# A hybrid decoder step on one core: weights loaded one unit earlier, and margins for steps in the planner of the side chains

## The chip, the cores and the metric

One core of a Trainium2 chip runs the whole program. The metric is the device time of one execution in microseconds, the median of several runs. The engines are TensorE (PE, with its weight loads shown apart as PEld), VectorE (DVE), ScalarE (ACT), GpSimd (POOL) and SyncE (SP), which issues all DMAs of this kernel in one queue.

## The reference

One step of a one-layer recurrent decoder is computed for 2048 prompt tokens and for 8 samples of 4 tokens, with 1024 channels, all in float32:

```
u   = LN(x) @ w_in                       # columns for four head groups
A: gated DeltaNet   (conv, delta rule, a triangular solve in each chunk)
B: Mamba-2 SSD      (conv, scalar decay)
C: HGRN2            (a decay per channel)
D: mLSTM            (running-max stabiliser)
h   = LN(alpha * x + concat(A, B, C, D) @ w_out)
out = LN(alpha * h + relu(h @ w_up)^2 @ w_down)
```

The recurrences A to D carry a state along the tokens and give it out at the end. All of it is exactly causal.

## The kernel before, in words

**The main line of work.** The prompt is cut into 4 blocks of 512 tokens; the 32 sample tokens ride along with block 0 in the input projection and with block 2 in the rest. `do_P` multiplies by w_in, block after block; `do_W` by w_out; `do_F` by w_up and w_down. Float32 accuracy comes from a split: weights and activations are each a high and a low half (fp32r), and three products are summed, high x high, low x high, high x low. A *unit* is 512 x 128 weights, 256 KB; there are 832 units. `w_get` issues the load of a unit into one of four `wraw` buffers, `w_split` makes its halves `whi` (mostly on ACT) and `wlo` (on POOL or DVE) in four buffers each, and `gemm` runs 4 x 3 matmuls with them (twice as many with sample tokens). `w_pump`, called before each unit, keeps loads and splits ahead: loads up to unit `cur + 4`, splits up to `cur + 2`.

**The side chains.** Beside the main line run generators, and each `yield` in them ends a step. `mix_stream("a")` runs `gen_A` for chunk after chunk of 128 tokens, `mix_stream("b")` runs `gen_B`, `gen_C`, `gen_D` in turn; `ln` streams make the layer norms and load the mixed results (`y_pre`); and each finished projection has an evacuating generator (`u_conv`, `u_gate` and others). A job of a mix stream begins in `begin`, with the loads of its inputs (`laA`, `laC`, `kzA`, `kzD`); the next job can begin at the mark `"pre"` of the one before it.

In `gen_A`, the inverse of 32 x 32 diagonal blocks is made by 31 steps on POOL (`a`, then `x32`), each with a row of the block that is broadcast to all partitions. The rows go to DRAM (`ud32d`) and come back in eight loads of four rows each into two `nb` buffers (`fetch`). After them, a product with the mask `bd32` on DVE puts the result into `X`, and PE transposes `X`. In `gen_C`, `level` runs for seven sizes in a staggered way: differences of the log decays on DVE, an exponential on ACT, products `qz` (in `kzD`) and `e_` on DVE, and a matmul of the two on PE.

**What sets the order.** The program is written out in one order by a planner, and each engine runs its queue in that order. The planner is the class `_Sim`: it holds a clock for each engine, estimates the time of each instruction when it is written, and knows when each tile is ready by this estimate; `move` does the same for a DMA, with one issue after another and a time to land. `gemm` calls `R.tick()` after every third matmul (or pair). `tick` lets a generator make its next step if its `ready` time is not later than PE's clock plus a slack (both slacks are negative, -0.25 and -0.3). `ready` is the latest estimated end of what the generator's last step wrote; `R.hold(us)` puts it later. Streams make no step while DVE's or ACT's clock is more than `BACK` (2.0) us ahead of PE's. `R.until` lets the chains go on without the main line, where the main line needs their result.

`tvp(n, late)` chooses POOL for an operation if POOL's estimated end is before the later of DVE's estimated end and PE's clock plus `late`; `cpv` chooses between ACT and DVE in the same way. In `w_split` they are called with `LATE_W` and `LATE_W - 1.0`, where `LATE_W` is 5.0.

The lines that record an instruction are one helper's (L341), so the profile's groups tell instructions apart by their tiles; DMAs have L470.

Of the kernel before, what the change touches and what calls it, by code (L numbers as in the profile page):

```python
# [39 lines left out]
EARLY_W = 3  # L40
SLACK = -0.25
SLACK_E = -0.3
BACK = 2.0
LATE_W = 5.0
LATE_U = 3.0
LN1_PACE = 0.1
W0_AT = 29
# [202 lines left out]
class _Run:  # L250
# [56 lines left out]
    def tick(self, fast=False):  # L307
        self.moved = False

        def ok(g, slack):  # L310
            return fast or g.ready <= self.clock["pe"] + slack
        live, self.evac = self.evac, []
        keep = [g for g in live if not ok(g, SLACK_E) or self._adv(g)]
        self.evac = keep + self.evac
        for q in self.streams.values():
            c = self.clock
            if not fast and max(c["dve"], c["act"]) > c["pe"] + BACK:
                break
# [36 lines left out]
def _ap(x):  # L355
    return x[:] if callable(x.ap) else x
# [85 lines left out]
def kernel(ctx: ExitStack, tc: tile.TileContext, t):  # L442
    nc = tc.nc
    R = _Run()
# [21 lines left out]
    mult, add, sub = ALU.mult, ALU.add, ALU.subtract  # L466
    vmax, vmin = ALU.max, ALU.min

    def dma(out, in_):
        nc.sync.dma_start(out=out, in_=in_)  # L470
        R.op("dma", R.sim.move(_ap(out), _ap(in_)))

    def A(out, in_, func, scale=1.0, bias=0.0):
        S.activation(out=out, in_=in_, func=func, scale=scale, bias=bias)
# [10 lines left out]
    def tt(out, a, b, op, eng=None):  # L485
        (eng or V).tensor_tensor(out=out, in0=a, in1=b, op=op)
# [27 lines left out]
    def bc1(ap, n):  # L514
        a = ap.unsqueeze(1)
        return a.to_broadcast([ap.shape[0], n] + list(ap.shape[1:]))
# [102 lines left out]
    units = []  # L619
    wst = {"nload": 0, "nsplit": 0, "cur": 0, "turn": 0}  # L620
    raws, his = {}, {}

    def w_get(i):
        w = sb4.tile([128, 4, 128], F32, tag="wraw", name="wraw")
        dma(w, units[i])
        raws[i] = w

    def w_pump():
        cur = wst["cur"]
        while wst["nload"] < min(cur + 5, len(units)):  # L630
            i = wst["nload"]
            w_get(i)
            wst["nload"] += 1
            if wst["nsplit"] < min(cur + 3, wst["nload"]):
                w_split()
        while wst["nsplit"] < min(cur + 3, len(units)):
            w_split()

    def w_split():
        i = wst["nsplit"]  # L640
        w = raws.pop(i)
        hi = sb4.tile([128, 4, 128], F32R, tag="whi", name="whi")
        lo = sb4.tile([128, 4, 128], F32R, tag="wlo", name="wlo")
        cpv(hi, w, 512, LATE_W - 1.0)
        tt(lo, w, hi.bitcast(F32), sub, tvp(512, LATE_W))
        his[i] = (hi, lo)
        wst["nsplit"] += 1
# [657 lines left out]
    def pa():  # L1305
        return psa.tile([128, 512], F32, tag="a", name="pa_")
# [16 lines left out]
    def gen_A(m):  # L1323
# [22 lines left out]
        p = pa()  # L1346
# [28 lines left out]
        if not dec:  # L1375
            ud = ta1(4, 32)
            V.tensor_reduce(out=ud, in_=X.rearrange("p h (b r) -> p h r b", r=32), axis=AX.X, op=add)
            V.tensor_copy(x32, bc1(C("id32", 32), 4))
            yield
            dma(ud32d, ud.rearrange("p h r -> p (h r)"))  # L1380
            yield
            rows = ud32d.rearrange("(b k) c -> b k c", k=32)
            nb = {}

            def fetch(q):
                if q < 8:
                    nb[q] = nbp.tile([128, 4, 4, 32], F32, tag="nb", name="nb")
                    dma(nb[q].rearrange("p k h r -> p (k h r)"), rows[:, 4 * q:4 * q + 4].rearrange("b k c -> b (k c)").unsqueeze(1).to_broadcast([4, 32, 512]))

            for q in range(NBUF):  # L1390
                fetch(q)
            yield
            tf = ta1(4, 31)
            for k in range(31):
                w_ = 31 - k
                tt(tf[:, :, 0:w_], nb[k // 4][:, k % 4, :, k + 1:], x32[:, :, k:k + 1].to_broadcast([128, 4, w_]), mult, G)
                tt(x32[:, :, k + 1:], x32[:, :, k + 1:], tf[:, :, 0:w_], sub, G)
                if k % 4 == 3:
                    yield
                if k % 4 == 3:  # L1400
                    fetch(k // 4 + NBUF)
            xb = x32.unsqueeze(2).to_broadcast([128, 4, 4, 32])
            tt(X.rearrange("p h (b r) -> p h b r", r=32), xb, bc1(C("bd32", 128).rearrange("p (b r) -> p b r", r=32), 4), mult, tvp(512))
            yield
# [194 lines left out]
    def gen_C(m):  # L1599
# [14 lines left out]
        p = pb()  # L1614
# [19 lines left out]
        def level(li, s):  # L1634
            e_ = tb1(2, 128)
            for i in range(2):
                evi = e_[:, i, 0:n].rearrange("p (b e s) -> p b e s", e=2, s=s)
                gvi = la[:, 2 + i, 0:n].rearrange("p (b e s) -> p b e s", e=2, s=s)
                gm = gvi[:, :, 0, s - 1]
                tt(evi[:, :, 0, :], bcf(gm, s), gvi[:, :, 0, :], sub, tvp(64))  # L1640
                tt(evi[:, :, 1, :], gvi[:, :, 1, :], bcf(gm, s), sub, tvp(64))
            yield
            ex(e_[:, :, 0:n], e_[:, :, 0:n])
            yield
            qz = kzD[:, :, 64 * (li % 2):64 * (li % 2) + 64].rearrange("p (i h) r -> p i h r", i=2)
            qv = la[:, 0:2, 0:n].rearrange("p i (b e s) -> p i b e s", e=2, s=s)
            ev = e_[:, :, 0:n].rearrange("p i (b e s) -> p i b e s", e=2, s=s)
            for h in range(2):
                sl = slice(64 * h, 64 * h + 64)
                tt(qz[sl, :, h, 0:nh].rearrange("p i (b s) -> p i b s", s=s), qv[sl, :, :, 1, :], ev[sl, :, :, 1, :], mult)  # L1650
            tt(e_[:, :, 0:n], k_, e_[:, :, 0:n], mult)
            yield
            pl = pb()
            for i in range(2):
                if n == 128:
                    mm(pl[:, i * 128:i * 128 + 128], e_[:, i, :], qz[:, i])
                else:
                    for h in range(2):
                        mm(pl[:n, (2 * i + h) * nh:(2 * i + h) * nh + nh], e_[:, i, 0:n], qz[:, i, h, 0:nh])
            yield  # L1660
            pv = pl[:n, 0:4 * nh].rearrange("p (h b s) -> p h b s", h=4, s=s)
            av = at[:n, :, 0:n].rearrange("p h (b e s) -> p h b e s", e=2, s=s)[:, :, :, 1, :]
            if s == 64:
                V.tensor_copy(av[0:64], pv[0:64])
            else:
                mk = bc1(C("lmc", nh, 64 * li, n).bitcast(U32), 4).rearrange("p h (b s) -> p h b s", s=s)
                V.copy_predicated(out=av, mask=mk, data=pv)
# [129 lines left out]

    def mix_stream(which):
        fns = (gen_A,) if which == "a" else (gen_B, gen_C, gen_D)
        jobs = []  # L1800
        for b in range(NB):
            for c, dec in [(c, False) for c in range(CPB)] + ([(0, True)] if b == DECB else []):
                for f in fns:
                    mark = None
                    if f is fns[-1]:
                        if dec:
                            mark = ("x", which)
                        elif c == CPB - 1:
                            mark = (b, which)
                    jobs.append((b, c, dec, f, mark))  # L1810

        def begin(i):
            b, c, dec, f, mark = jobs[i]
            m = chunk(b, c, dec)

            def store(k, y):
                def go(ready):
                    R.cur.ready = ready
                    R.hold(1.0)
                    yield  # L1820
                    dma(m.yT[:, k:k + 2, :], y[:, :, 0:m.n])
                    if mark:
                        done["mix"].add(mark)
                R.start(go(R.cur.ready))

            m.store = store
            g = _Task(f(m))
            g.ready = R.cur.ready
            R._adv(g)
            return g  # L1830

        def fed(i):
            g = {gen_A: "A", gen_B: "B", gen_C: "C", gen_D: "D"}[jobs[i][3]]
            return left[jobs[i][0]][""] == left[jobs[i][0]][g] == 0

        nxt = None
        for i in range(len(jobs)):
            g = nxt
            nxt = None
            if g is None:  # L1840
                while not fed(i):
                    yield
                g = begin(i)
            R.cur.ready = max(R.cur.ready, g.ready)
            yield
            for mark in g.gen:
                if mark == "pre" and i + 1 < len(jobs) and fed(i + 1):
                    nxt = begin(i + 1)
                yield
        if which == "a":  # L1850
            dma(t["pa_ssm"], SA)
        else:
            dma(t["pb_ssm"], SB)
            dma(t["pc_ssm"], SC)
            dma(t["pd_mem"], SD)
# [418 lines left out]
```

## Time and profile before

| | |
|---|---|
| median of 3 runs | 3063.7 us (3060.96 to 3063.87) |
| profiled execution | 3063.81 us |
| its span, first to last instruction | 3061.9 us |
| mean granted TensorE clock | 0.983 |
| busy: PE, PEld | 2889.6 us, 2480.4 us |
| busy: DVE, POOL, ACT | 2141.5 us, 1621.9 us, 1260.7 us |
| instructions: PE, DVE, ACT, POOL | 16668, 4038, 2685, 1993 |
| DMA | 407.12 MB, mean 133 GB/s |
| splits: wlo on POOL, on DVE; whi on ACT, on DVE | 769, 63; 829, 3 |

A busy PE counts the modelled end of each matmul, so it is not PE at its peak. Idle time is the gap before an instruction, put down to what released it; only PE's idle time is certain to be part of the time. The input projection of block 3 ends near 1000 us with the first output projection; the side chains run from about 150 to 2290 us; after that PE has the main line alone but for layer norms.

### The profile page before, as it was taken

Reading aid. Unit: us, or ns where it says so; the run is one execution under the profiler, and the core shown is the slowest. Engines: PE = TensorE matmul, PEld = TensorE weight load, DVE = VectorE, ACT = ScalarE, POOL = GpSimd, SP = SyncE. Lnnn points to the kernel's source line nnn. Section 1 sums busy time; section 2 is a strip of 40 time slices with the busy share of each in tenths; the row PEclk is TensorE's granted clock in tenths of the full one; section 3 lists DMA queues with packets and bytes.
Section 4 is the critical chain, followed back from the end, with each engine's and each line's share of the span. In section 5 each row is a group of like instructions: output and inputs, shape, how many; then the busy total and the mean of one; then the engine's idle time right before and its main releaser. Section 6 shows DMA issues by size and latency. Waiting matters only on the chain.

```text
span 3061.9 us, 48064 instructions
## 1 busy us (share of the span) xinstructions
PE 2889.6 (94%) x16668; PEld 2480.4 (81%) x16668; DVE 2141.5 (70%) x4038; ACT 1260.7 (41%) x2685; POOL 1621.9 (53%) x1993
## 2 busy tenths in 40 slices
PE   7889898999999999999999999999999999999997
PEld 7788677777777787877777778878899999878886
DVE  8677796978897687877778766767684354474445
ACT  4654565574564433333335222333542222432222
POOL 4554756585685464466443654453344444444545
PEclk9899999999999999999999999999999999999999
DMA  5775446456557444345443444444333343333333
GB/s 166 127 172 153 141 147 205 138 157 185 157 144 214 130 134 138 118 135 155 134 145 89 144 127 129 135 141 137 112 109 94 86 119 86 111 112 97 100 93 104
DMA packets 361264, 407.12 MB, mean 133 GB/s; under 512 B 65468, under 2 KB 207804, under 8 KB 361020
## 3 DMA queue, kind: packets, MB, share of 16 engines
q1 hardware_dynamic: 361020, 404.04, 46.3%
q8 instruction: 132, 2.16, 0.3%
q14 instruction: 112, 0.92, 0.1%
HBM read 340.20 MB, written 63.72 MB: 132 GB/s over the span
## 4 chain that ended last, share of the span: by engine, by line
PE 48%; DVE 20%; POOL 11%; DMA 11%; issue 6%; ACT 4%; SPq 1%; POOLq 0%; DVEq 0%; ACTq 0%
PE pd L341 40%; DVE g L341 10%; DMA nb<-ud32d 5%; POOL wlo L341 4%; DVE b L341 4%; POOL a L341 3%; POOL x L341 3%; DVE a L341 2%; ACT g L341 2%; DMA wraw<-in_w_in_u_dram 2%; DVE kzD L341 2%; SPq L470 1%; DMA wraw<-in_w_up_u_dram 1%; DMA prx<-in_a_conv_in_dram 1%; POOL g L341 1%
## 5 line engine op out<-in xcount | busy, mean ns | idle before, releaser
L341 PE MATMUL pd<-g,whi 128*128 128x512 f32 (+2 forms) x8112 | 2243.7, 361 | 21.2 <-ACT g L341 11.3
L341 POOL TENSOR_TENSOR wlo<-wraw,whi 128x512 fp32r<-128x512 f32 x769 | 1066.0, 1394 | 1236.7 <-ACT whi L341 1139.3
L341 PEld LDWEIGHTS pd<-g,whi 128*128 128x128 f32 x8112 | 1395.3, 190 | 223.5 <-ACT g L341 12.4
L341 PE MATMUL pd<-g,wlo 128*128 128x512 f32 (+2 forms) x4056 | 1310.5, 354 | 18.7 <-POOL wlo L341 18.0
L341 PEld LDWEIGHTS pd<-g,wlo 128*128 128x128 f32 x4056 | 723.3, 191 | 114.7 <-POOL wlo L341 27.0
L341 ACT ACTIVATE whi<-wraw 128x512 fp32r<-128x512 f32 x829 | 509.4, 626 | 551.0 <-PE pd L341 249.7
L341 DVE TENSOR_TENSOR g<-g 128x512 fp32r<-128x512 f32 (+5 forms) x371 | 368.7, 997 | 199.0 <-ACT g L341 190.1
L341 ACT ACTIVATE g<-pd 128x512 f32<-128x512 f32 (+1 forms) x342 | 174.1, 527 | 495.9 <-PE pd L341 494.2
L341 DVE TENSOR_TENSOR g<-g,pd 128x512 f32<-128x512 f32 (+2 forms) x288 | 159.5, 570 | 221.7 <-PE pd L341 221.0
L341 POOL TENSOR_TENSOR a<-nb,x 128x124 f32<-128x124 f32 (+30 forms) x496 | 201.7, 407 | 97.9 <-DMA nb<-ud32d 68.8
L341 ACT ACTIVATE g<-g 128x512 f32<-128x512 f32 (+5 forms) x343 | 210.0, 633 | 67.6 <-DVE g L341 60.0
L341 POOL TENSOR_TENSOR x<-x,a 128x124 f32<-128x124 f32 (+30 forms) x496 | 197.2, 398 | 38.9
L341 DVE CAST g<-g 128x512 fp32r<-128x512 f32 (+1 forms) x169 | 173.2, 1025 | 7.8 <-ACT g L341 3.0
L341 ACT ACTIVATE b<-b 128x256 f32<-128x256 f32 (+3 forms) x201 | 81.3, 405 | 166.9 <-DVE b L341 166.2
L341 DVE TENSOR_TENSOR b<-laC 128x64 f32<-128x64 f32 (+2 forms) x471 | 117.4, 307 | 9.6 <-DMA laC<-UC 9.6
L341 DVE SCALAR_TENSOR_TENSOR g<-g 128x512 f32<-128x512 f32 (+3 forms) x124 | 111.5, 905 | 17.7 <-ACT g L341 15.4
L341 DVE SCALAR_TENSOR_TENSOR g<-g,par 128x512 f32<-128x512 f32 (+1 forms) x128 | 117.5, 934 | 1.2 <-ACT g L341 1.1
L341 DVE TENSOR_TENSOR kzD<-laC,b 64x128 f32<-64x128 f32 (+1 forms) x228 | 108.4, 475 | 2.0 <-ACT b L341 0.3
L341 DVE BATCH_NORM_STATS2 bst<-g 128x6 f32<-128x512 f32 (+1 forms) x98 | 65.7, 683 | 44.4 <-ACT g L341 40.9
L341 DVE TENSOR_SCALAR g<-g 128x512 int32<-128x512 int32 (+7 forms) x137 | 72.9, 550 | 32.9 <-ACT g L341 32.1
L341 POOL TENSOR_TENSOR g<-g 128x512 f32<-128x512 f32 (+3 forms) x47 | 70.2, 1497 | 43.7 <-ACT g L341 38.9
L341 DVE TENSOR_TENSOR wlo<-wraw,whi 128x512 fp32r<-128x512 f32 x63 | 52.1, 828 | 53.4 <-ACT whi L341 53.1
(2536 smaller groups left out, 2738.0 us busy)
## 6 DMA issues: line engine op xcount, KB each, us to landing
wraw<-in_w_dn_u_dram SPq DMA_DIRECT2D x264, 256.0 KB
wraw<-in_w_up_u_dram SPq DMA_DIRECT2D x256, 256.0 KB
wraw<-in_w_in_u_dram SPq DMA_DIRECT2D x248, 256.0 KB
nb<-ud32d SPq DMA_DIRECT2D x128, 256.0 KB
wraw<-in_w_out_u_dram SPq DMA_DIRECT2D x64, 256.0 KB
UC<-g SPq DMA_DIRECT2D x40, 256.0 KB
g<-in_x_prompt_dram SPq DMA_DIRECT2D x32, 256.0 KB
hTd<-g SPq DMA_DIRECT2D x32, 256.0 KB
```

What stands on the lines that cost most here:

```text
L341: r = f(*a, **k)
L470: nc.sync.dma_start(out=out, in_=in_)
```

## The change

Six places change, and none of them adds or removes arithmetic.

- `w_pump` loads up to unit `cur + 5` instead of `cur + 4`. The `wraw` buffers stay four.
- `LATE_W` goes from 5.0 to 3.0, so a weight's halves go to DVE where POOL's (ACT's) estimated end is more than 3.0 (2.0) us behind PE's clock, and later than DVE's.
- `dma` can add time to the landing estimate; `fetch` uses it with 3.2 us for the `nb` rows.
- After the 31 steps of `gen_A` stands `R.hold(SWEPT)`, 2.0 us, and one more `yield`, before the product that needs the result.
- In `level` of `gen_C`, `R.hold(BUSY)`, 0.7 us, stands before the step with the matmul.
- In `begin`, the job's `ready` is put 1.5 us (`LOADED`) later after its loads are issued.

```
+LOADED = 1.5
+SWEPT = 2.0
+BUSY = 0.7
-LATE_W = 5.0
+LATE_W = 3.0
...
-    def dma(out, in_):
+    def dma(out, in_, extra=0.0):
         nc.sync.dma_start(out=out, in_=in_)
-        R.op("dma", R.sim.move(_ap(out), _ap(in_)))
+        R.op("dma", R.sim.move(_ap(out), _ap(in_), extra))
...
-        while wst["nload"] < min(cur + 5, len(units)):
+        while wst["nload"] < min(cur + 6, len(units)):
...
-                    dma(nb[q]..., rows[...]...to_broadcast([4, 32, 512]))
+                    dma(nb[q]..., rows[...]...to_broadcast([4, 32, 512]), 3.2)
...
                 if k % 4 == 3:
                     fetch(k // 4 + NBUF)
+            R.hold(SWEPT)
+            yield
             xb = x32.unsqueeze(2).to_broadcast([128, 4, 4, 32])
...
             tt(e_[:, :, 0:n], k_, e_[:, :, 0:n], mult)
+            R.hold(BUSY)
             yield
             pl = pb()
...
             g = _Task(f(m))
             g.ready = R.cur.ready
             R._adv(g)
+            g.ready += LOADED
             return g
```

More of the change, by code (lines that the diff above doesn't have):

```diff
@@ L1387, in fetch @@
                     nb[q] = nbp.tile([128, 4, 4, 32], F32, tag="nb", name="nb")
-                    dma(nb[q].rearrange("p k h r -> p (k h r)"), rows[:, 4 * q:4 * q + 4].rearrange("b k c -> b (k c)").unsqueeze(1).to_broadcast([4, 32, 512]))
+                    dma(nb[q].rearrange("p k h r -> p (k h r)"), rows[:, 4 * q:4 * q + 4].rearrange("b k c -> b (k c)").unsqueeze(1).to_broadcast([4, 32, 512]), 3.2)
             for q in range(NBUF):
```

## The prediction

> **What bounds the kernel now.** I read the page's busy shares first, then a table of busy time by stage, then who waited for whom, engine by engine.
>
> ```profile
> 250.00:950.00 700.00, 653.12 (x3312) 533.57 (x3312) 582.41 (x1109) 406.59 (x847) 447.79 (x578) 0.98 0.55 158
> 950.00:1600.00 650.00, 617.07 (x3302) 508.25 (x3302) 486.62 (x1009) 243.57 (x567) 338.33 (x526) 0.99 0.49 143
> 1600.00:2285.00 685.00, 658.28 (x3895) 555.42 (x3895) 501.58 (x1094) 255.09 (x572) 322.52 (x430) 0.99 0.42 123
> 2285.00:2650.00 365.00, 365.00 (x2748) 356.80 (x2747) 167.12 (x215) 92.35 (x181) 175.35 (x128) 1.00 0.36 105
> ```
>
> Each row is a stretch of the span, with its length, the busy time of PE, PEld, DVE, ACT and POOL in that order, then the granted clock. PE is the bound. After 2285 us, when the side chains are through, it is never idle (365.0 of 365.0). While they run it loses 47, 33 and 27 us in the three stretches. Everything that the change touches lies in those stretches, so its whole scope is PE's waits there and the clock that the waits cost. PE has no slack anywhere: a wait taken off PE comes off the span, one added goes on.
>
> The waits show which steps were put into the engines' queues too early.
>
> ```profile
> PEld pd L341 <- POOL wlo L341: 27.0, 23, 3.3
> POOL a L341 <- DMA nb<-ud32d: 68.8, 28, 6.7
> DVE a L341 <- POOL x L341: 51.5, 15, 8.0
> ACT whi L341 <- DMA wraw<-in_w_up_u_dram: 78.1, 29, 9.2
> ACT whi L341 <- DMA wraw<-in_w_in_u_dram: 69.8, 29, 6.5
> ACT whi L341 <- DMA wraw<-in_w_dn_u_dram: 66.1, 24, 6.8
> ACT whi L341 <- DMA wraw<-in_w_out_u_dram: 24.8, 10, 5.3
> SPq L470 <- POOL wlo L341: 938.9, 414, 9.8
> ```
>
> Each row gives total us, times, longest. POOL stands 68.8 us before a recursion step because the broadcast rows (nb) have not landed; the low weight halves (wlo) that are queued behind it come late, and PE's weight loads wait 27.0 us for them. DVE stands 51.5 us at the product that follows the recursion. ACT stands 238.8 us in 92 waits (the four wraw rows) for weights still on their way. The order of time shows one such case from end to end:
>
> ```profile
> 1401.25 0.40 POOL L341 TENSOR_TENSOR a<-nb,x 128x124 f32<-128x124 f32 x1 [6.72 <-DMA nb<-ud32d]
> ...
> 1404.97 1.26 POOL L341 TENSOR_TENSOR wlo<-wraw,whi 128x512 fp32r<-128x512 f32 x1
> ...
> 1406.28 0.29 PEld L341 LDWEIGHTS pd<-g,wlo 128*128 128x128 f32 x1 [3.32 <-POOL wlo L341]
> ...
> 1406.90 0.63 ACT L341 ACTIVATE whi<-wraw 128x512 fp32r<-128x512 f32 x1 [8.66 <-DMA wraw<-in_w_up_u_dram]
> ```
>
> POOL waits 6.72 us for nb, runs the segment, does wlo only at 1404.97, and PE loses 3.32 us. ACT waits 8.66 us for a weight at the same time.
>
> **The change, part by part.** No arithmetic is added or removed; the order of instructions in the queues changes. All sums are against the profiled execution: 3063.8 us, of which 3061.9 are span; the median of the runs is 3063.7, so no correction is needed.
>
> *Margin of 3.2 us for nb, 2.0 us and one more step after the recursion, and splits moved from POOL to DVE two us sooner.* These three aim at PE's wait for wlo, 27.0 us, and at the transposes after the recursion. With the nb margin the planner puts each segment into POOL's queue up to 3.2 us later; 68.8 us in 28 waits are 2.5 us each, so little should be left, and the wlo behind it come earlier. The transposes' share, and that of the late loads below, is in these rows:
>
> ```profile
> PE pa__22049 L341 <- DVE a L341: 2.8, 1, 2.8
> PE pa__8981 L341 <- DVE a L341: 2.0, 1, 2.0
> PE pa__20962 L341 <- DVE a L341: 1.6, 1, 1.6
> PE pa__10472 L341 <- DVE a L341: 1.1, 1, 1.1
> PE pb__13377 L341 <- DMA laC<-UC: 3.1, 1, 3.1
> PE pb__2960 L341 <- DMA laC<-UC: 2.9, 1, 2.9
> PE pb__12345 L341 <- DMA laC<-UC: 1.3, 1, 1.3
> ```
>
> The first four add up to 7.5 us. Bounds for wlo: nothing gained (0) to all 27.0; I take two thirds, 18, since a margin of 3.2 covers the mean of those waits but not the longest, 6.7. For the transposes 0 to 7.5; I take 6, since the margin of 2.0 alone covers three of the four waits. The cost: each recursion gets later in its chain. That chain hides it (below).
>
> *LOADED, 1.5 us at a job's start.* The last three rows are PE's waits for laC, 7.3 us; a margin of 1.5 takes 1.5 + 1.5 + 1.3 = 4. Bounds 0 and 7.3.
>
> *BUSY, 0.7 us before the level products of gen_C.*
>
> ```profile
> L341 DVE TENSOR_TENSOR kzD<-laC,b x228: 216/290/1429, 251.3 to 2240.1; 64x128 f32<-64x128 f32 x112, 64x32 f32<-64x32 f32 x2
> ...
> its engine sat idle before it (us, times) until:
>   DVE b L341: 31.5, 33
> ...
> PE pb__17982 L341 <- DVE b L341: 2.9, 1, 2.9
> ```
>
> The answer for kzD counts the weight load and the matmul of one product separately, so PE's share of 31.5 us is about half, 16 us in some 17 waits, mean 0.95. A later issue by 0.7 takes at most 17 x 0.7 = 12; I take 10 (bounds 0 and 16).
>
> *The clock after these waits.*
>
> ```profile
> 2041.00:2044.00 3.00, 0.63 (x3) 0.19 (x1) 1.39 (x1) 1.63 (x3) 2.61 (x8) 1.00 0.13 48
> 2044.00:2050.80 6.80, 6.41 (x23) 5.79 (x24) 3.80 (x7) 1.39 (x3) 3.13 (x2) 0.52 0.45 114
> 1350.00:1358.00 8.00, 6.12 (x38) 4.84 (x37) 7.86 (x20) 1.90 (x4) 2.54 (x2) 1.00 0.15 52
> 1358.00:1361.00 3.00, 3.00 (x11) 2.55 (x10) 1.76 (x5) 0.00 (x0) 0.00 (x0) 0.52 0.00 0
> 1644.60:1651.40 6.80, 6.80 (x23) 5.39 (x22) 6.61 (x18) 3.79 (x7) 2.01 (x2) 0.52 0.05 20
> ```
>
> The wait of 2.8 us at 2041 is followed by 6.8 us at a clock of 0.52; so are the waits within 1350 to 1358, all for kzD (3.0 us), and the 2.9 us of pb__17982 before 1644.6 (6.8 us). Half of these 16.6 us, 8, is lost to the clock; with two thirds of the waits gone, 6 come back. Bounds 0 and 8. The Trainium skill, "TensorE: Matmul & The Clock Gate", section "What's actually happening", has the array return to half rate only after about 3.4 us of idle window. By that rule waits this short cost no clock, and the sum below would be 6 us smaller in its gain; the trace disagrees, since between 1350 and 1358 PE was busy 6.12 of 8 us and the clock halved all the same.
>
> *Weights one unit further ahead.* There are four wraw buffers, so the load can't start before the low half four units back is done; what changes is its place in SP's queue, ahead of the other transfers of one unit. It helps where such a transfer held it up, as in ACT's 8.66 us above. Directly PE pays little for it; I take 3 us, bounds 0 and 10 (the price of the other small waits here), as ACT's evacuations come sooner. The price: the transfers of that unit (stores, loads of the chains, nb) now stand behind a load that waits for a later wlo. SP's 938.9 us behind wlo should rise to well over 1500. Bounds 0 and 10; I take 3.
>
> *Splits on DVE.*
>
> ```profile
> L341 POOL TENSOR_TENSOR wlo<-wraw,whi x769: 1255/1297/2282, 15.2 to 3042.2; 128x512 fp32r<-128x512 f32 x193
> L341 DVE TENSOR_TENSOR wlo<-wraw,whi x63: 673/746/1816, 17.5 to 2006.2; 128x512 fp32r<-128x512 f32 x63
> DVE wlo L341 <- ACT whi L341: 53.1, 29, 7.0
> 250.00:950.00 700.00, 290.48 (x752) 141.77 (x752) 19.25 (x24) 230.26 (x158) 0.98 0.55 158
> L341 POOL TENSOR_TENSOR a<-nb,x x496: 207/342/1978, 190.7 to 2042.1; 128x124 f32<-128x124 f32 x6, 128x112 f32<-128x112 f32 x6, 128x100 f32<-128x100 f32 x6, 128x88 f32<-128x88 f32 x6
> ```
>
> I expect 63 to become 120 to 200, at 0.75 us of DVE instead of 1.30 us of POOL. Queued behind it on DVE are PSUM evacuations, and PE waits for those; I take 4 us (bounds: -3, as POOL gets freer, and 50, the rival below). The Trainium skill, "SBUF — State Buffer", section "SBUF: two separate sides", says that a GpSimd operation and a VectorE operation with two SBUF inputs lock each other out for the whole instruction. By that rule a split on DVE frees POOL of only 1.30 - 0.75 = 0.55 us and the term of 18 would be nearer 12, the gain 6 smaller; a maximum of 1978 ns against a median of 342 for the recursion's products agrees with such blocking.
>
> *What hides the longer chains.* The margins lengthen the chains, in the second by up to 7 levels x 0.7 us for 12 jobs = 59 us plus part of 39 x 1.5 = 58 by the sample group.
>
> ```profile
> L470 SPq DMA_DIRECT2D yTx<-b x3: 376/377/378, 1777.5 to 1914.4; - x3
> L470 SPq DMA_DIRECT2D g<-yTx x8: 320/430/528, 1980.8 to 1999.8; - x8
> L470 SPq DMA_DIRECT2D wraw<-in_w_out_u_dram x2: 328/374/419, 2108.6 to 2110.0; - x2
> ```
>
> Its last store is at 1914.4; the projection that needs it starts at 2108.6, and loading it took 20 us. About 170 us of lateness are covered; the chains' end at 2285 has a longer cover still, the PE-only stretch. So I cost it at 0; without cover, each us late would be a us of idle PE.
>
> **Sum.** Gains 18 + 6 + 4 + 10 + 6 + 3 = 47. Costs 3 + 4, and 12 (a quarter of the gain) for waits that come next: where one late input is mended, the next (ACT's evacuation of g) is the one that PE meets, = 19. Net 28: 3063.8 - 28 = 3036 us.
>
> **Rivals.**
> *The gain is larger.* Longer chains thin out DVE in 250 to 950, where it is busy 582 of 700 us; 47 us of PE idle there fall as a whole, not only where a margin is. With half of the 107 us of idle in the three stretches gone plus the clock's 8, 61 us: 3003. For it: DVE's share; against: nothing shortens any operation.
> *The waits only move.* All queues are in order, and each shifted step meets other work. Then some 45 of the 47 come back as new waits: 3062, within 3057 to 3069. For it: most PE waits are single events under 3 us, at many places.
> *DVE becomes the bound: slower.* In 250 to 950 it has 700 - 582.4 = 117.6 us free. A moved split takes 0.83 us plus, by the row, 53.1 / 63 = 0.84 of waiting for its high half: 1.67. From 117.6 / 1.67 = 70 moved there (of 158) it decides. With 100 moved, 167 - 118 = 49 us are added against the 28: 3063.8 + 21 = 3085. Against: the planner moves a split only when its own DVE clock is the earlier one.
> *Chains too late for the third block: slower.* Over 170 us of delay needed, I count at most 117; at 200 us PE would idle 30 us, against the 28: 3066.
>
> **Chances.** Forecast 0.56, larger gain 0.11, waits only move 0.16, DVE bound 0.13, chains late 0.04. A measurement can tell about 0.2%, 6 us, from no change. Faster takes the first two and 0.07 of the third: 0.74; same 0.08; slower 0.18. The likeliest case by itself spans 3015 to 3052; the range of 3000 to 3070 leaves out the far part of the larger gain and most of the DVE case, together about 2 in 10.
>
> **What would show it.** Right: POOL's wait for nb from 68.8 to under 20, DVE's for POOL x from 51.5 to under 20, PEld for wlo from 27.0 to under 12, the kzD row from 31.5 to under 18, ACT for wraw from 238.8 to under 170, DVE splits above 120, SP behind wlo above 1500, the last yTx store between 1950 and 2050. PE busy falls little, its idle time falls. Wrong: DVE above 620 us in 250 to 950, PE waits for DVE g or ACT g in place of wlo, or PE idle before the projection near 2100.

## The result, and the profile after

The changed kernel takes 3031.0 us (median of 4 runs, 3030.7 to 3038.8), the kernel before 3063.6: the ratio is 0.9901, with a 95% interval of 0.9887 to 0.9915. Forecast were 3036 us and 3000 to 3070. The sum came out; several of its terms did not.

The busy shares of the page, and the stretches of the span as they were shown before (length; busy PE, PEld, DVE, ACT, POOL; granted clock):

```profile
PE 2873.8 (95%) x16668; PEld 2472.5 (82%) x16668; DVE 2167.6 (72%) x4104; ACT 1249.1 (41%) x2658; POOL 1592.5 (53%) x1958
...
250.00:950.00 700.00, 664.59 (x3406) 545.54 (x3405) 601.94 (x1151) 411.01 (x863) 430.95 (x547) 0.99 0.58 166
950.00:1600.00 650.00, 619.15 (x3312) 513.48 (x3311) 499.46 (x1076) 249.88 (x573) 332.72 (x546) 0.98 0.48 139
1600.00:2285.00 685.00, 664.19 (x4068) 565.34 (x4067) 511.81 (x1055) 243.55 (x543) 335.15 (x434) 1.00 0.44 127
```

The profiled execution spans 3028.4 us after 3061.9, so 33.5 less. PE's idle time went from 3061.9 - 2889.6 = 172.3 to 3028.4 - 2873.8 = 154.6, so 17.7 of the 33.5 is idle time; the other 15.8 us is time in which PE counted as busy, though it ran the same 16668 matmuls. The granted clock accounts for at most about 7 us of that (0.017 x 3062 = 52 us were lost to it before, 0.015 x 3028 = 45 after); the rest was not traced. Between 250 and 950 us, PE is idle for 35 us in place of 47.

The waits, in the order of the rows shown before; the first two rows are PE's own waits for wlo, before and after:

```profile
PE pd L341 <- POOL wlo L341: 18.0, 16, 2.9
PE pd L344 <- POOL wlo L344: 3.7, 4, 1.4
PEld pd L344 <- POOL wlo L344: 6.1, 7, 1.8
PEld pd L344 <- DVE wlo L344: 3.2, 3, 1.9
POOL a L344 <- DMA nb<-ud32d: 71.9, 39, 5.0
DVE a L344 <- POOL x L344: 2.6, 3, 1.6
ACT whi L344 <- DMA wraw<-in_w_up_u_dram: 23.5, 11, 4.6
ACT whi L344 <- DMA wraw<-in_w_in_u_dram: 21.1, 8, 6.4
ACT whi L344 <- DMA wraw<-in_w_out_u_dram: 4.1, 1, 4.1
SPq L473 <- POOL wlo L344: 1226.3, 484, 8.4
```

PE's weight loads wait 6.1 us for wlo from POOL, not 27.0, and PE itself 3.7 us, not 18.0. ACT's waits for weights on their way fell from 238.8 us to 48.7 in these rows (51.0 with w_dn). DVE's stand before the product after the recursion, 51.5 us, is gone; the planner now gives 4 of the 16 products to POOL. POOL's wait for nb, which the nb margin was to remove, is as long as before, 71.9 us against 68.8. And SP stands behind wlo for 1226 us in place of 939, as the deeper loads have it, though not for the "well over 1500" that was forecast.

### The profile page after: what moved, and what is told of

It reads as the page before. It is cut to its first block, busy times and chain, and to the rows that moved or that the text cites. A ratio compares the mean times of both kernels' runs of the same rounds, so it can differ in the third digit from the quotient of the medians.

```text
span 3028.4 us, 48058 instructions
## 1 busy us (share of the span) xinstructions
PE 2873.8 (95%) x16668; PEld 2472.5 (82%) x16668; DVE 2167.6 (72%) x4104; ACT 1249.1 (41%) x2658; POOL 1592.5 (53%) x1958
## 5 line engine op out<-in xcount | busy, mean ns | idle before, releaser
L344 POOL TENSOR_TENSOR wlo<-wraw,whi 128x512 fp32r<-128x512 f32 x710 | 992.7, 1405 | 1218.5 <-ACT whi L344 1089.9
L344 PEld LDWEIGHTS pd<-g,whi 128*128 128x128 f32 x8048 | 1380.6, 189 | 206.6 <-DVE g L344 9.1
L344 ACT ACTIVATE whi<-wraw 128x512 fp32r<-128x512 f32 x813 | 498.8, 626 | 363.0 <-PE pd L344 257.4
L344 DVE TENSOR_TENSOR g<-g 128x512 fp32r<-128x512 f32 (+5 forms) x364 | 357.2, 985 | 177.0 <-ACT g L344 163.5
L344 POOL TENSOR_TENSOR a<-nb,x 128x124 f32<-128x124 f32 (+30 forms) x496 | 199.0, 401 | 101.6 <-DMA nb<-ud32d 71.9
L344 POOL TENSOR_TENSOR x<-x,a 128x124 f32<-128x124 f32 (+30 forms) x496 | 208.2, 420 | 38.9
L344 DVE CAST g<-g 128x512 fp32r<-128x512 f32 (+1 forms) x178 | 187.0, 1051 | 10.2 <-POOL g L344 3.2
L344 DVE TENSOR_TENSOR wlo<-wraw,whi 128x512 fp32r<-128x512 f32 x122 | 95.9, 787 | 55.9 <-ACT whi L344 55.4
L344 DVE SCALAR_TENSOR_TENSOR g<-g 128x512 f32<-128x512 f32 (+3 forms) x124 | 99.5, 805 | 18.9 <-ACT g L344 18.5
```

The source lines that it names most:

```text
L344: r = f(*a, **k)
```

## The experiments

The kernel before was run beside every one; the ratios are to it, and the times are medians. The last four columns are totals of waits in the profile, in us: DVE for POOL's recursion result (x), POOL for nb, ACT for wraw, PEld for wlo from POOL.

| kernel | us | ratio, 95% interval | DVE: x | POOL: nb | ACT: wraw | PEld: wlo |
|---|---|---|---|---|---|---|
| before | 3061.5 to 3064.3 | 1 | 51.5 | 68.8 | 238.8 | 27.0 |
| before, slack -0.27 | 3095.8 | 1.0114 (1.0096 to 1.0132) | 65.5 | 98.0 | 238.2 | 37.1 |
| + load depth | 3096.6 | 1.0104 (1.0085 to 1.0124) | 73.1 | 88.9 | 77.6 | 38.4 |
| + LATE_W | 3132.0 | 1.0218 (1.0192 to 1.0243) | 74.3 | 101.2 | 226.9 | 18.9 |
| + LOADED, BUSY | 3086.9 | 1.0075 (1.0053 to 1.0098) | 50.2 | 48.9 | 244.4 | 23.8 |
| + recursion margins | 3046.0 | 0.9937 (0.9918 to 0.9955) | 0.4 | 13.2 | 149.8 | 17.2 |
| the same, slack -0.27 | 3032.6 | 0.9902 (0.9884 to 0.9919) | 0.4 | 18.8 | 155.3 | 17.7 |
| changed | 3031.0 | 0.9901 (0.9887 to 0.9915) | 2.6 | 71.9 | 51.0 | 6.1 |
| changed, slack -0.27 | 3024.7 | 0.9881 (0.9863 to 0.9898) | 2.5 | 50.8 | 41.7 | 4.1 |
| - load depth | 3037.8 | 0.9921 (0.9905 to 0.9936) | 4.8 | 34.5 | 165.0 | 10.7 |
| - recursion margins | 3130.0 | 1.0229 (1.0209 to 1.0249) | 86.4 | 152.5 | 69.6 | 23.1 |
| - SWEPT alone | 3032.2 | 0.9897 (0.9882 to 0.9913) | 27.0 | 53.8 | 44.2 | 8.2 |
| - nb margin alone | 3055.9 | 0.9971 (0.9956 to 0.9987) | 9.7 | 127.2 | 93.8 | 18.5 |
| changed, nb margin 4.8 | 3003.7 | 0.9805 (0.9788 to 0.9821) | 2.8 | 45.9 | 69.6 | 6.1 |

DVE can wait only for the products that the planner leaves on it: all 16 in the kernels without the hold and in the last one, 7 to 13 in the others.

### One part at a time, on the kernel before

**Load depth alone.**

```diff
-        while wst["nload"] < min(cur + 5, len(units)):
+        while wst["nload"] < min(cur + 6, len(units)):
```

> The kernel before with one edit: loads five units ahead of the running one in place of four. Theory A (most of the 32 us comes through the weights: ACT's waits for wraw fell from 238.8 us to under 60, PE's for wlo from 27.0 to 6.1): 3044 us, between 3036 and 3052; ACT's waits for wraw under 100 us, PEld's for wlo under 15, and the second chain ends before 2284. Theory B, the prediction's split of the gain (3 of 47 us for this part): 3061 to 3066, and SP's longer waits behind wlo show no gain. Theory C (any new order of the same work moves the time by several us either way): no tie between ACT's waits for wraw and the time.

Measured: 3096.6 us, 32 slower. ACT's waits for wraw fell as theory A said, to 77.6 us, and the time rose all the same; the waits of PEld for wlo rose:

```profile
PEld pd L341 <- POOL wlo L341: 38.4, 34, 3.2
POOL a L341 <- DMA nb<-ud32d: 88.9, 42, 5.9
DVE a L341 <- POOL x L341: 73.1, 16, 8.7
```

So ACT's waits for weights do not set the time by themselves, and theory A falls; theory C's "no tie" holds. Theory B's near zero did not come either, but 32 us is no more than an edit that means nothing costs this kernel (below), so they can't be put down to the loads. The second chain ended later, not sooner.

**LATE_W alone.**

```diff
-LATE_W = 5.0
+LATE_W = 3.0
```

> The kernel before with LATE_W 3.0 in place of 5.0 alone. Theory A: 3050 to 3058, wlo on DVE above 100 and PEld's waits for wlo under 18 us. Theory B: a third of the 18 us, 3056 to 3060, less the 4 us for DVE. Theory C: anything from 3054 to 3072.

Measured: 3132.0 us, 68 slower, outside what all three theories gave. The splits moved as expected, 118 wlo on DVE, and PEld's waits for wlo fell to 18.9, just above theory A's 18; but POOL stood 101.2 us for nb and DVE 74.3 us for x, and PE's own waits for DVE's tiles (a, b, g) rose from 59.8 to 119.1 us.

**The recursion's margins alone.**

```diff
-                    dma(nb[q]..., ...to_broadcast([4, 32, 512]))
+                    dma(nb[q]..., ...to_broadcast([4, 32, 512]), 3.2)
...
                     fetch(k // 4 + NBUF)
+            R.hold(2.0)
+            yield
```

> The kernel before with the nb margin of 3.2 and the hold with the extra step after the recursion, alone. Theory B: 3045 to 3052, POOL's waits for nb from 68.8 us to under 20, PEld's for wlo under 15. Theory A: 3058 to 3066; POOL's waits for nb stay near 70 us as they did with the whole change, DVE's waits for POOL x go from 51.5 us to under 10, without a gain on PE.

Measured: 3046.0 us, 18 faster: the one part that gains by itself, in theory B's range.

```profile
PEld pd L341 <- POOL wlo L341: 17.2, 18, 2.1
POOL a L341 <- DMA nb<-ud32d: 13.2, 14, 2.7
...
L341 DVE TENSOR_TENSOR a<-x,con x12: 673/682/1741, 256.0 to 2042.5; 128x512 f32<-128x512 f32 x12
```

POOL's waits for nb fell to 13.2 us as the prediction had it; PEld's for wlo, 17.2, stayed above theory B's 15. The third row is the product after the recursion (min/median/max ns); four of the 16 went to POOL.

**LOADED and BUSY alone.**

```diff
             tt(e_[:, :, 0:n], k_, e_[:, :, 0:n], mult)
+            R.hold(0.7)
...
             R._adv(g)
+            g.ready += 1.5
```

> The kernel before with LOADED 1.5 and BUSY 0.7 alone. Theory B: 14 us for the two plus their clock, 3047 to 3053, the waits of the kzD answer from 31.5 us to under 18. Theory A: 3056 to 3064; the kzD waits fall by half, and others rise.

Measured: 3086.9 us, 23 slower, outside both. The kzD answer has 36.8 us of waits for DVE b, more than the 31.5 of before.

### Is it only the order that was drawn?

The four groups of edits give +32, +68, -18 and +23, a sum of +105, and together -32. So either the parts need each other, or each order is a draw. To tell these apart, an edit that means nothing was run on both kernels.

**The streams' slack, on the kernel before.**

```diff
-SLACK = -0.25
+SLACK = -0.27
```

> The kernel before with the streams' slack at -0.27 in place of -0.25: no margin that means anything, but about 60% of the listed PE rows change place. Theory C: 10 us or more away from 3064, either way. Theory D and the prediction's: within 6 us of 3064, since no step's margin is changed by more than 0.02 us.

Measured: 3095.8 us, 34 slower. An edit of 0.02 us in the planner's arithmetic costs as much as the whole change gained. That is theory C for the kernel before. Its 3064 us look like a favourable order: the five other kernels without the recursion's margins take 3087 to 3132.

**The same edit on the changed kernel.**

> The changed kernel with the streams' slack at -0.27 in place of -0.25. Theory C: 10 us or more away from 3031, and rather slower, if the changed kernel's order is a lucky draw. Theory D: within 6 us of 3031.

Measured: 3024.7 us, 6 faster. This other order cost the changed kernel nothing; neither theory C's "rather slower" nor its 10 us hold.

**The changed kernel without the deeper loads.**

```diff
-        while wst["nload"] < min(cur + 6, len(units)):
+        while wst["nload"] < min(cur + 5, len(units)):
```

> The changed kernel with the load depth put back (four units ahead), all else as changed. The single edits gave +32 us (load depth), +68 (LATE_W), -18 (recursion), +23 (begin and level margins), a sum of +105 where the whole gave -32, so the parts are not additive. Theory D (the parts need each other: the deeper loads take ACT's waits for wraw from 238.8 us to about 80 whatever else is changed, and this pays once the recursion's margins keep POOL free): without the loads 3060 or more, ACT's waits for wraw above 180 us. Theory C (each new order draws a time from a spread of some 20 us, whatever the edit): anything between 3025 and 3090, with no tie to ACT's waits.

Measured: 3037.8 us, ACT's waits for wraw back at 165.0. Theory D's 3060 fails, and so does its 180: some 7 us hang on the load depth here, about what the slack alone moved.

**The changed kernel without the recursion's margins.**

```diff
-                    dma(nb[q]..., ...to_broadcast([4, 32, 512]), 3.2)
+                    dma(nb[q]..., ...to_broadcast([4, 32, 512]))
...
-            R.hold(SWEPT)
-            yield
```

> The changed kernel without the nb margin and without the hold and step after the recursion. Theory D: 3075 or more, DVE's waits for POOL x back above 40 us, POOL's for nb above 85, PEld's for wlo above 20. Prediction's split: 24 us of the gain lost plus clock, 3055 to 3062. Theory C: anything between 3025 and 3090.

Measured: 3130.0 us, 99 slower than with them.

```profile
PEld pd L341 <- POOL wlo L341: 23.1, 16, 3.7
POOL a L341 <- DMA nb<-ud32d: 152.5, 72, 6.5
DVE a L341 <- POOL x L341: 86.4, 16, 10.3
```

All of theory D's signs for this run came, and the time lies outside theory C's spread and the prediction's split. The nb and x rows are back, larger than before; PEld's for wlo, 23.1, stays a little under its 27.0. DVE's mean wait at the product is 86.4 / 16 = 5.4 us, and everything behind it on DVE waits along. PE is idle for 60.6 us more than in the changed kernel. Some 28 us of that are its waits for the transposes right behind the product (31.9 against 3.4), 13 its waits for wlo, and 20 its waits for DVE's b, the tiles of the second chain.

### Which of the two margins

**Without the hold and step after the recursion.**

```diff
-            R.hold(SWEPT)
-            yield
```

> The changed kernel without the hold and step after the recursion; the nb margin stays. Theory E (the price is paid by DVE standing at the product until POOL has ended the recursion, 51 to 86 us in every kernel without the two margins and under 5 in every one with them, and the nb margin does most of it, since it adds up over eight loads): 3028 to 3050, DVE's waits for POOL x under 25 us. Theory G (the step after the recursion does it): 3070 to 3110, DVE's waits for POOL x above 40. Theory C (a drawn order): no tie to DVE's waits for POOL x.

Measured: 3032.2 us, the same as with it; DVE's waits for x are 27.0 us, just above theory E's 25. This speaks against theory E's mechanism: all 16 products are on DVE here, with a median of 1724 ns, DVE stands 24 us more than in the changed kernel, and the time is the same.

**Without the nb margin.**

```diff
-                    dma(nb[q]..., ...to_broadcast([4, 32, 512]), 3.2)
+                    dma(nb[q]..., ...to_broadcast([4, 32, 512]))
```

> The changed kernel without the nb margin; the hold and step after the recursion stay. Theory E: 3075 to 3125, DVE's waits for POOL x above 35 us and POOL's for nb above 100. Theory G: 3028 to 3050, DVE's waits for POOL x under 20. Theory C: as before, no tie.

Measured: 3055.9 us, 25 slower than the changed kernel; between theory G's 3028 to 3050 and theory E's 3075 to 3125, which asked for DVE waits above 35 where there were 9.7 (nine of the 16 products went to POOL). So each of the two alone takes most of the 99 us (98 and 74). The nb margin takes both waits down (nb from 152.5 to 53.8, x from 86.4 to 27.0); the hold takes down DVE's (to 9.7) and little of POOL's (to 127.2). The faster of the two is the one in which DVE stands longer, so the time does not follow DVE's standing by itself. Theory E had the nb margin's place right and its exclusive share wrong.

**The recursion's margins alone, with the other slack.** The edit of the third run above, and `SLACK = -0.27`.

> The kernel before with the two recursion margins, as in the run of these alone (3046), and with the streams' slack at -0.27 in place of -0.25, which by itself took the kernel before from 3062 to 3096. Theory E: the margins also steady the time; within 10 us of 3046, so some 50 under the kernel before with the same slack. Theory C: 3060 or more, or under 3030.

Measured: 3032.6 us, 63 under the kernel before with the same slack (3095.8); 13 from 3046, so a little outside theory E's 10. With the margins, the two slacks gave 3046 and 3033, and with the whole change 3031 and 3025; without them 3064 and 3096.

**A wider nb margin in the changed kernel.**

```diff
-                    dma(nb[q]..., ...to_broadcast([4, 32, 512]), 3.2)
+                    dma(nb[q]..., ...to_broadcast([4, 32, 512]), 4.8)
```

> The changed kernel with an nb margin of 4.8 in place of 3.2 us. POOL's waits for nb were 71.9 us in the changed kernel, with the deeper loads, against 13.2 with the recursion margins alone. Theory E: POOL's waits for nb under 30, DVE's for POOL x about 0, 3020 to 3032, hardly faster since PE's waits for wlo are only 6 us by now. Theory C: 3015 to 3050.

Measured: 3003.7 us, ratio 0.9805 (0.9788 to 0.9821): faster than both kernels by far more than expected.

```profile
PEld pd L344 <- POOL wlo L344: 6.1, 6, 1.8
POOL a L344 <- DMA nb<-ud32d: 45.9, 26, 5.0
1600.00:2285.00 685.00, 672.41 (x4195) 579.64 (x4194) 508.87 (x1058) 242.44 (x540) 349.31 (x482) 1.00 0.45 132
```

PEld's waits for wlo are no smaller; POOL's for nb fell by a third only. PE is busy 672 of 685 us in the third stretch, against 664. How much of these 27 us is the margin and how much the order is open: the other kernels with both margins differ by up to 21 us.

## Why the prediction was right, step by step

**The sum.** 28 us were forecast and 32.5 measured. PE's idle time fell by 17.7 us; that its busy time would fall only little was wrong, it fell by 15.8. By what PE itself waited for, 47 us of waits went and 29 us of new ones came, where the sum had gains of 47, 6 of them the clock's, and costs of 19. The places are other ones, though. Of the 47 that went, 14.3 are wlo, 5.6 the transposes and 2.3 laC, as forecast, but 14.2 are ACT's a, which the sum has only within the 3 us for the loads (11.1 of them went without the deeper loads too); of the 29, 11.6 are laA and 12.8 DVE's a at other places than these transposes. And the terms were added as if they were independent, and the single runs show that they are not. So the total fits in good part by luck. Of the signs asked for, three did not come: POOL's wait for nb under 20, SP's above 1500 and the later last yTx store.

**The recursion's margins, 18 + 6 us.** The waits aimed at are the right ones. The bound of 27.0 for wlo was PEld's row, which is not PE's idle time; PE's own wait was 18.0, so the 18 was all of it, and 14.3 came (with LATE_W and the loads; 7.3 with the margins alone). PE's waits at the transposes right behind the product were 9.0 us and are 3.4, so the 6 came too. But the margins are worth more than these rows of the kernel before show: alone they gave 18 us, against the kernel before with the other slack 63, within the whole 99. What the step missed is how much longer the same places stand in other orders. PE's own waits for DVE's a, b and g are 47 to 62 us in all kernels with one or both margins, 59.8 in the kernel before, and 74 to 119 in the five others without. That DVE's late evacuations and gen_C products, behind its stand at the product, are the way there fits the run without both margins but not the run without the hold alone, so it is argued, not shown. What POOL does next makes the product itself take longer. The product itself, before and after (min/median/max ns):

```profile
L341 DVE TENSOR_TENSOR a<-x,con x16: 655/1747/1770, 248.5 to 2042.6; 128x512 f32<-128x512 f32 x16
L344 DVE TENSOR_TENSOR a<-x,con x12: 681/690/1814, 256.6 to 2015.3; 128x512 f32<-128x512 f32 x12
```

Before, it starts when POOL ends the recursion, which is when POOL starts what is queued behind, mostly a wlo: POOL's operation begins 0.05 to 0.09 us ahead of it, and the product takes 1747 ns in the median. Seven products of the changed kernel take 0.68 or 0.69 us. Four of them meet no POOL operation; beside the other three it is POOL's operation that takes longer, 1.70 and 1.81 us where it began 0.15 and 0.02 us after the product, and 2.80 us in the third case. The Trainium skill, "SBUF — State Buffer", section "SBUF: two separate sides", says that a VectorE operation with two SBUF inputs and a GpSimd one hold each other off for their whole length; the 1.06 us more agree with it. With the wait, one product in the kernel before cost DVE some 3.2 + 1.06 us, 16 times; what of that reaches PE is less, as the run without the hold shows.

The step "little should be left" of POOL's 68.8 us failed in the changed kernel (71.9) and held alone (13.2). With LATE_W as changed and the margins in, it is 34.5 us without the deeper loads and 71.9 with them. That the loads ahead in SP's queue hold up nb would fit; it was not isolated.

**Weights further ahead, 3 against 3.** Zero was forecast, 32 slower alone and 7 faster within the whole were measured. ACT's waits fell from 238.8 to 51.0 us with little effect on the time: an engine that is not the bound stood less. The price named, transfers standing behind a load that waits for wlo, would fit one place in the trace:

```profile
165.20 1.12 PE L344 MATMUL pa__1954<-con,laA 128*128 128x128 f32 x4 [12.15 <-DMA laA<-UA]
...
160.00:165.00 5.00, 0.00 (x0) 0.00 (x0) 0.00 (x0) 0.00 (x0) 0.00 (x0) 0.50 0.85 136
165.00:172.00 7.00, 6.80 (x35) 6.80 (x36) 2.84 (x9) 3.00 (x9) 1.34 (x2) 0.59 0.91 161
```

PE waits 12.2 us for the first chunk's laA, and the granted clock over the next 7 us is 0.59. A wait of PE for the first laA, 5.8 to 12.8 us, stands in the profile of all seven kernels with the deeper loads; in the seven with the old depth the longest wait for laA is 1.1 us. But it stands largely in place of other waits: in the kernel before, PE waits 7.5 us for ACT's a in the same chunk (pa__2055), a row that is gone. Up to 250 us both kernels run 1488 matmuls (the changed one fewer of the main line and more of the chains), with PE idle for 45.8 us before and 48.2 after. With the deeper loads alone it was 55.2. So the price stayed within its 0 to 10, and its 3 can't be told from nothing.

**Splits on DVE, cost 4.** 63 became 122, within 120 to 200; DVE is busy 602 us between 250 and 950, under the 620 that would have made it the bound. The rival of a DVE bound fell for the changed kernel; and with the nb margin of 4.8 DVE is busy 623 us there in the fastest kernel of all, so the 620 was no sign of harm. LATE_W alone cost 68 us, but with DVE busy 2156 us in all, hardly more than before, and 567 in that stretch: the extra waits are at nb and x, so a full DVE is not the cause; how that loss divides between the order and the recursion's stands was not separated.

**LOADED and BUSY, 4 + 10.** The kzD waits nearly halved in the whole, and rose alone:

```profile
its engine sat idle before it (us, times) until:
  issue: 20.1, 20
  DVE b L344: 16.4, 20
```

31.5 to 16.4 us is the forecast "under 18", but that is luck: the row does not follow the margin. With the two parts alone it was 36.8 us, with 23 us of loss; in the changed kernel without the deeper loads it is 33.4, and with the recursion's margins and the other slack, without BUSY, 16.0. PE's own waits for DVE's b went from 36.3 only to 34.5, so the 10 did not come there; its waits for laC went from 7.5 to 5.2, so of the 4 some 2 came. What LOADED and BUSY bring within the whole was not run by itself.

**All four parts beside the recursion's margins.** They bring 0.9937 to 0.9901 at one slack, and 0.9902 to 0.9881 at the other, where the intervals overlap: 6 to 11 us, about what the slack alone moves.

**The clock, 6.** The granted clock went from a mean of 0.983 to 0.985, which is 0.002 x 3030 = 6 us. The size fits, but executions of the kernel before differ more than that among themselves (0.979 to 0.989), and which waits gave it was not traced.

**The chains.** Forecast was a later last yTx store, between 1950 and 2050. It came at 1809.8, and the chain's last output at 2173.7, where it was 2284.3:

```profile
L473 SPq DMA_DIRECT2D yTx<-b x3: 377/378/597, 1680.7 to 1809.8; - x3
L473 SPq DMA_DIRECT2D out_pd_mem_dram<-SD x1: 442/442/442, 2173.7 to 2173.7; - x1
```

This step of the prediction failed, harmlessly. LATE_W goes with it: that output comes at 2107 to 2255 us in all kernels with LATE_W 3.0 and at 2284 to 2364 in all with 5.0. A likely way is that fewer splits in the planner's ACT queue let the streams step more often under the BACK rule; this was only argued.

## What to carry to other kernels

In a kernel whose order comes from a planner, first change something that means nothing (0.02 us of slack) and see how far the time moves; here that was 34 us without the recursion's margins, and 6 and 13 with them, so a single edit's run says little by itself. Look first at the step in which an in-order engine stands still for another engine's long chain, even if that engine is not the bound: margins at DVE's 51.5 us of standing and POOL's 68.8 were worth 18, 63 and 99 us in three comparisons; the loads that took over 100 us off ACT's waits brought no gain alone and 7 us in the whole. Which of the two waits carries the price stays open, since either margin alone took most of it. In the runs here the two margins also made the time steadier against the other edits: 3025 to 3046 us in five kernels that have both, at 3.2 us for nb, and 3064 to 3132 in six that have neither.

## What the runs showed of the hardware

The product of 128 x 512 on DVE took 0.68 or 0.69 us in the changed kernel where POOL ran nothing or began just after it, and 1747 ns in the median in the kernel before, where a POOL operation of the same size began 0.05 to 0.09 us ahead of it. I had not expected an engine at 70% busy to be delayed so much by a start at the same time as another's; here a wait of 3.2 us for POOL brought 1.06 us more, as both went on at once.
